# Attention that normalises its outputs instead of its probabilities, and adds its band mask in the scores' own number type, in a two-layer hybrid backbone

## The chip, the core and the metric

The kernel runs on one core of a Trainium2 chip. A core has a matrix engine (PE in the profile, with PEld for its weight loads), a vector engine (DVE), a scalar engine (ACT), a general engine (POOL) and a queue engine for transfers (SP). Each engine works through its own list of instructions in the order in which the program wrote them, and waits for the others by semaphores. The metric is the time of one execution in device microseconds (us); less is better.

## The reference, cut to what matters

The program computes two layers over 256 latent and 256 context tokens with 1024 features. Both mix tokens by attention with 64 features per head: the first layer with 8 query heads (beside a state-space branch, S5), the second with 16 query heads in a band of 128 positions, with a sink logit per head that takes part in the sum of the softmax alone. What the change touches is the softmax with its values:

```
def gqa_scores(q5, k):
    s = jnp.einsum('bqkgd,bskd->bkgqs', q5, k, preferred_element_type=jnp.float32)
    return s * (HEAD_DIM ** -0.5)

def gqa_values(p, v):
    return jnp.einsum('bkgqs,bskd->bqkgd', p.astype(v.dtype), v)

def sink_softmax(s, sink):
    sk = jnp.broadcast_to(sink.astype(jnp.float32)[:, :, None, None], s.shape[:-1] + (1,))
    p = jax.nn.softmax(jnp.concatenate([s, sk], axis=-1), axis=-1)
    return p[..., :-1]
...
    valid = (kpos >= 0) & (kpos < n) & (jnp.abs(kpos - qpos) <= WINDOW)
    ...
        s_loc = jnp.where(mi, gqa_scores(qi, ki), -jnp.inf)
```

## The kernel before, in words

Nearly all large products are done three times, on halves of a split: a number is kept as a rounded high part (type fp32r) and a remainder, and `mm3` (L390) multiplies high by high, high by low and low by high. The program runs feed-forward, mixer, feed-forward for each layer. Weights come by transfers on SP, and ACT and DVE split them (L281, L299) one use ahead. The order on each engine is the order in which the Python code writes instructions; there is no scheduler. Pieces of side work are generators in a list `bg`, and each call of `tick()` writes the next piece of each.

**Attention** (L915) is called twice, with 8 units each. A unit is 128 queries and two neighbouring query heads for each of two key heads; its two key heads are its two subs, so there are 16 subs. A loop of steps handles sub after sub, with stages three steps apart. At step s it writes:
- `scores` of sub s: for two heads a product with the high and one with the low part of the keys (L934, L937), into one of four buffers of the accumulator memory, and in the second layer between them a bf16 product of an identity with a mask of 128 columns (L936); then a maximum on DVE (L938);
- `transposes` of sub s-3 on PE (L985), copied out by ACT (L986);
- `softmax` of sub s: the maximum scaled on DVE (L950), two exponentials on ACT with their sums (L958); then, for sub s-1, the inverse of the sums on DVE (L970) and the scaling of the two probability tiles: in the first layer one on ACT (L973) and one on POOL (L975), in the second one on DVE and one on POOL (both L975);
- `values`, at each odd step from 5 on, of the unit whose two subs are transposed: products of values and probabilities into `po` (L995), whose result DVE copies and splits into high and low part, head by head (L999, L1000);
- `tick()`, which in the first layer brings the S5 branch: products on PE (L1469, L1546), a rotation on POOL (L1497 to L1503), scans and products on DVE (L1514 to L1528), copies on ACT (L1472, L1557).

The context queries of the first layer see 256 keys, all others 512, so that a tile of scores there is 256 columns wide for subs 0 to 7 and 512 for the rest. After the attention comes the output projection (`pwo`).

The mask tiles are made once, early in the program, on POOL (`win_masks`, L821). The second layer's mixer (`mixer_win`, L1758) begins with products for keys and values (`pkv`), while the norm of its input is still being made: ACT, DVE and POOL write the operand tiles `hh` and `hl` feature block by feature block, and POOL raises the mean squares to the power -1/2 (L530), which PE spreads over the partitions (L534).

Of the kernel before, what the change touches and what calls it, by code (L numbers as in the profile page):

```python
# [11 lines left out]
F32 = mybir.dt.float32  # L12
# [24 lines left out]
def hybrid_kernel(ctx: ExitStack, tc: tile.TileContext, x, c, ctx_in, c_ctx, mod_w, mod_b, norm_g, ffn_wg, ffn_wu,  # L37
# [66 lines left out]
    def ps(name, tag="mm", shape=(128, 512)):  # L104
        return psum.tile(list(shape), F32, name=name, tag=tag, bufs={"mm": 4, "tp": 2, "ms": 2}[tag])

    def tt(name, shape, tag=None, bufs=2, dtype=F32):
        return tmp.tile(list(shape), dtype, name=name, tag=tag or name, bufs=bufs)
# [58 lines left out]
    class Operand:  # L167
# [11 lines left out]

        def __getitem__(self, ix):  # L180
            return self.t[ix[2] // 4][ix[:2] + (ix[2] % 4,) + ix[3:]]

    hh, hl = Operand("hh"), Operand("hl")

# [3 lines left out]
    def tokens(t):  # L188

        return t // 2, slice((t % 2) * 128, (t % 2 + 1) * 128)  # L190
# [624 lines left out]
                G.tensor_mul(ropeS[:, z, :, hs], rp[:, :, 32:64], gains[:, l, z, None, ho].to_broadcast([128, 2, 32]))  # L815
            G.tensor_scalar(ropeS[:, z, :, 0:32], ropeS[:, z, :, 0:32], -1.0, None, op0=OP.mult)

    masks = const.tile([128, 3, 128], BF16, name="masks")
    sinkb = const.tile([128, 2, 16], F32, name="sinkb")

    def win_masks():  # L821

        mf = tt("mf", [128, 2, 128], tag="half", bufs=3)
        G.memset(mf, 0.0)
        G.affine_select(mf[:, 0], mf[:, 0], pattern=[[-1, 128]], base=0, channel_multiplier=1,
                        compare_op=OP.is_ge, fill=NEG)
        G.affine_select(mf[:, 1], mf[:, 1], pattern=[[1, 128]], base=0, channel_multiplier=-1,
                        compare_op=OP.is_ge, fill=NEG)
        G.tensor_copy(masks[:, 0:2], mf)
        G.tensor_copy(masks[:, 2], ident)  # L830
        G.tensor_scalar(sinkb[:, 1], sinkb[:, 0], -1.0, None, op0=OP.mult)

    scr = const.tile([128, 1], F32, name="scr")

# [80 lines left out]
    def attention(ap, units, qT, rq, kTh, kTl, v, dst, pt_slots, mask=None, sinkb=None):  # L915


        subs = [(u, kvl) for u in range(len(units)) for kvl in range(2)]
        state = {}
        pt_n = [0]  # L920

        def scores(u, kvl):
            qcol, kvp, hg0, nkb, msk = units[u]
            nk = nkb * 128
            kv = kvp * 2 + kvl
            l = 0 if sinkb is None else 1
            assert ("q", l, (kv * 4 + hg0) // 8 * 8, qcol.start) in ready
            assert all(("k", l, b * 128) in ready for b in range(nkb))
            scs = []
            mx = tt("mx", [128, 8], bufs=3)  # L930
            for i in range(2):
                h = kv * 4 + hg0 + i
                sc = ps("sc")
                T.matmul(sc[:, 0:nk], qT[:, h, qcol], kTh[:, kv, 0:nk], start=True, stop=False)  # L934
                if msk is not None:
                    T.matmul(sc[:, msk[1] * 128:(msk[1] + 1) * 128], mask[:, 2], mask[:, msk[0]], start=False, stop=False)  # L936
                T.matmul(sc[:, 0:nk], qT[:, h, qcol], kTl[:, kv, 0:nk], start=False, stop=True)  # L937
                V.tensor_reduce(mx[:, i:i + 1], sc[:, 0:nk], axis=AX.X, op=OP.max)  # L938
                scs.append(sc)
            state[u, kvl] = [scs, mx, None]  # L940

        def softmax(u, kvl, prev):

            if (u, kvl) in state:
                qcol, kvp, hg0, nkb, msk = units[u]
                nk = nkb * 128
                scs, mx, _ = state[u, kvl]
                hs = slice((kvp * 2 + kvl) * 4 + hg0, (kvp * 2 + kvl) * 4 + hg0 + 2)
                rqu = rq[:, qcol.start // 128]
                V.tensor_mul(mx[:, 2:4], mx[:, 0:2], rqu[:, 1, hs])  # L950
                if sinkb is not None:
                    V.tensor_tensor(mx[:, 2:4], mx[:, 2:4], sinkb[:, 1, hs], op=OP.min)
                    G.tensor_add(mx[:, 4:6], mx[:, 2:4], sinkb[:, 0, hs])
                sm = tt("smx", [128, 8], bufs=3)
                P = []
                for i in range(2):
                    p = xt_("P", [128, 512])
                    S.activation(p[:, 0:nk], scs[i][:, 0:nk], AF.Exp, bias=mx[:, 2 + i:3 + i],  # L958
                                 scale=rqu[:, 0, hs.start + i:hs.start + i + 1],
                                 accum_out=sm[:, i:i + 1])  # L960
                    P.append(p)
                if sinkb is not None:
                    S.activation(sm[:, 2:4], mx[:, 4:6], AF.Exp)
                state[u, kvl] = [P, sm]
            if prev in state:
                P, sm = state[prev]
                nk = units[prev[0]][3] * 128
                if sinkb is not None:
                    V.tensor_add(sm[:, 0:2], sm[:, 0:2], sm[:, 2:4])
                V.reciprocal(sm[:, 4:6], sm[:, 0:2])  # L970
                for i in range(2):
                    if sinkb is None and i == 0:
                        S.activation(P[i][:, 0:nk], P[i][:, 0:nk], AF.Copy, scale=sm[:, 4:5])  # L973
                        continue
                    (G if i else V).tensor_scalar(P[i][:, 0:nk], P[i][:, 0:nk], sm[:, 4 + i:5 + i], None, op0=OP.mult)  # L975

        def transposes(u, kvl):
            P, sm = state[u, kvl]
            nkb = units[u][3]
            pts = pt_slots[pt_n[0] % len(pt_slots)]  # L980
            pt_n[0] += 1
            for i in range(2):
                pt = ps("ppt", "tp")
                for kb in range(nkb):
                    T.transpose(pt[:, kb * 128:(kb + 1) * 128], P[i][:, kb * 128:(kb + 1) * 128], ident)  # L985
                S.copy(pts[:, 0:nkb, i * 128:(i + 1) * 128], pt[:, 0:nkb * 128].rearrange("p (b q) -> p b q", b=nkb))  # L986
            state[u, kvl] = pts

        def values(u):
            qcol, kvp, hg0, nkb, msk = units[u]  # L990
            po = ps("po", "ms")
            for kb in range(nkb):
                for kvl in range(2):
                    kv = kvp * 2 + kvl
                    T.matmul(po[kvl * 64:kvl * 64 + 64, 0:256], v[:, kb, kv * 64:kv * 64 + 64], state[u, kvl][:, kb, :],  # L995
                             start=kb == 0, stop=kb == nkb - 1, tile_position=(0, kvl * 64))
            for i in range(2):
                hi, lo = dst(u, i)
                V.tensor_copy(hi, po[:, i * 128:(i + 1) * 128])  # L999
                V.tensor_sub(lo, po[:, i * 128:(i + 1) * 128], hi.bitcast(F32))  # L1000

        n = len(subs)
        l = 0 if sinkb is None else 1
        TL, dp, sf = TLS[l], DP[l], SF[l]
        for s_ in range(n + TL):
            if s_ < n and sf:
                scores(*subs[s_])
            if s_ >= TL:
                transposes(*subs[s_ - TL])
            if s_ < n and not sf:  # L1010
                scores(*subs[s_])
            c_ = s_ - dp
            if 0 <= c_ <= n:
                softmax(*(subs[c_] if c_ < n else (-1, 0)), subs[c_ - 1] if c_ else None)
            if s_ >= TL + 2 and (s_ - TL) % 2 == 0:
                values(subs[s_ - TL - 2][0])
            tick()
        values(subs[n - 1][0])


# [12 lines left out]
    def s5_prep(pp):  # L1033
# [44 lines left out]
        for _ in range(6):  # L1078
            yield
        rope_tables(0)  # L1080
        win_masks()
        ee = pt_("ee", [128, 1])
        G.memset(ee, math.e)
        dP = pt_("dP", [32, 2])
# [338 lines left out]
    def mixer_ab(nm, ap, nxt):  # L1423
# [220 lines left out]
        for t in range(4):  # L1644
            s_, tl = tokens(t)
            pq = ps("pq")
            for i in range(2):
# [6 lines left out]
                if i:  # L1654
# [3 lines left out]

        units = [(slice(qt * 128, (qt + 1) * 128), 0, hg0, 4 if qt >= 2 else 2, None) for qt in range(4) for hg0 in (0, 2)]
        attention(ap, units, qT, rq, kTh, kTl, v,  # L1660
                  lambda u, i: tuple(z[:, u // 4, 4 + units[u][2] + i, tokens(u // 2)[1]] for z in (hh, hl)),
                  [z[:, s_] for z in (hh.renew(0, F32), hl.renew(0, F32)) for s_ in (CTX, LAT)])
        gc = ap.tile([128, 2, 2, 4, 256], F32R, name="gc", tag="big")

# [93 lines left out]
    def mixer_win(nm, ap, nxt):  # L1758
# [2 lines left out]
        v = ap.tile([128, 4, 256], F32, name="v1")  # L1761
        qT = ap.tile([128, 16, 256], F32R, name="qT1")
        rq = ap.tile([128, 2, 2, 16], F32, name="rq1")
        ckv = [use(("wkv", 0), pre=MW == 0 or WA == 0)]
        pk = [ps("pkv1") for _ in range(4)]
        for s_ in (CTX, LAT):
# [34 lines left out]
                        tick()  # L1801
        if WX:
            warm(AF.Exp)
        units = [(slice(qt * 128, (qt + 1) * 128), kvp, hg0, 4, (0, 3) if qt == 0 else (1, 2))
                 for kvp in range(2) for qt in range(2) for hg0 in (0, 2)]
        attention(ap, units, qT, rq, kTh, kTl, v,
                  lambda u, i: tuple(z[:, LAT, units[u][1] * 4 + units[u][2] + i, units[u][0]] for z in (hh, hl)),
                  [ap.tile([128, 4, 256], F32, name="pts%d" % i) for i in range(4)], mask=masks, sinkb=sinkb)
        fsl = [slice(0, 128), slice(128, 256)]
        for dp in range(4):  # L1810
# [169 lines left out]
```

## Time and profile before

| What | Value |
|---|---|
| time, median of 3 runs | 1765.51 us (1764.81 to 1765.52) |
| the profiled execution's own time | 1764.46 us |
| its span, first to last instruction | 1762.7 us |
| busy: PE, DVE, ACT, POOL | 1710.7, 1081.6, 633.7, 423.6 us |
| mean granted clock of PE | 0.984 of full speed |

A busy PE is not PE at its peak: matmuls overlap, so two starts one behind the other tell what a matmul costs, rather than its duration. The first attention lies at about 518 to 607 us of the span, the second at about 1479 to 1539 us.

### The profile page before, as it was taken

The numbers are of one execution on the slowest core, as the hardware profiler recorded it, in microseconds if no ns is written. First come the engines' busy times: TensorE is split into PE (matmuls) and PEld (weight loads), VectorE is DVE, ScalarE is ACT, GpSimd is POOL, SyncE is SP. The second block draws the span as 40 slices with busy tenths as digits, with TensorE's granted clock in tenths as the row PEclk, the third lists the DMA queues.
The fourth block names the chain that finished last, engine by engine and source line by source line (L and its number), as shares of the span: only waits on it lengthen the run. The fifth ranks groups of instructions, "written<-read, shape, count | busy, mean of one in ns | idle before, by whom it ended". The sixth has DMA issues, their size and how long they took to land.

```text
span 1762.7 us, 25223 instructions
## 1 busy us (share of the span) xinstructions
PE 1710.7 (97%) x9951; PEld 1432.0 (81%) x9951; DVE 1081.6 (61%) x1802; ACT 633.7 (36%) x1210; POOL 423.6 (24%) x565
## 2 busy tenths in 40 slices
PE   6999999999987999999999999999999998999998
PEld 4778888878975689888888898888888886699998
DVE  5565767666578755576556554754546378755455
ACT  3322222223445643222222243222222357754443
POOL 5314779322367303000000022000000046620000
PEclk8999999999998899999999999999999999999999
DMA  8546575596534524464445323554645224045653
GB/s 262 183 139 174 160 210 178 178 295 215 162 114 162 136 77 165 150 203 135 158 137 165 107 94 114 161 180 146 212 149 166 92 96 96 1 144 169 205 176 120
DMA packets 209453, 272.60 MB, mean 155 GB/s; under 512 B 23672, under 2 KB 171384, under 8 KB 208824
## 3 DMA queue, kind: packets, MB, share of 16 engines
q1 hardware_dynamic: 204912, 261.26, 47.0%
q10 hardware_dynamic: 3064, 5.32, 0.8%
q0 software_dynamic: 1360, 4.42, 0.8%
q8 instruction: 78, 1.28, 0.3%
q14 instruction: 39, 0.32, 0.1%
HBM read 255.77 MB, written 15.17 MB: 154 GB/s over the span
## 4 chain that ended last, share of the span: by engine, by line
PE 84%; DVE 7%; ACT 3%; DMA 3%; issue 2%; POOL 1%; SPq 0%; ACTq 0%; POOLq 0%; DVEq 0%
PE pu L391 16%; PE pu L392 15%; PE pu L393 15%; PE pd L391 7%; PE pd L392 6%; PE pd L393 6%; PE pwo L391 1%; PE pwo L393 1%; PE pwo L392 1%; PE pm L452 1%; PE pacc L391 1%; PE pacc L392 1%; PE pacc L393 1%; DVE H L1528 1%; PE po L995 1%
## 5 line engine op out<-in xcount | busy, mean ns | idle before, releaser
L391 PE MATMUL pu<-hh,whi 128*128 128x512 f32 (+1 forms) x1392 | 505.2, 363 | 1.5 <-ACT hh L548 1.1
L392 PE MATMUL pu<-hl,whi 128*128 128x512 f32 (+1 forms) x1392 | 500.7, 360 | 2.6 <-DVE hl L550 2.6
L393 PE MATMUL pu<-hh,wlo 128*128 128x512 f32 (+1 forms) x1392 | 500.2, 359 | 0.0
L299 DVE TENSOR_TENSOR wlo<-raw,whi 128x1024 fp32r<-128x1024 f32 (+2 forms) x314 | 358.2, 1181 | 42.5 <-ACT whi L281 42.1
L281 ACT CAST whi<-raw 128x1024 fp32r<-128x1024 f32 (+1 forms) x310 | 294.0, 998 | 244.4 <-PE pd L392 160.6
L391 PEld LDWEIGHTS pu<-hh,whi 128*128 128x128 f32 x1392 | 263.5, 189 | 49.6 <-issue 5.3
L392 PEld LDWEIGHTS pu<-hl,whi 128*128 128x128 f32 x1392 | 263.6, 189 | 41.2 <-DVE hl L550 3.4
L393 PEld LDWEIGHTS pu<-hh,wlo 128*128 128x128 f32 x1392 | 263.4, 189 | 39.3 <-DVE wlo L299 0.2
L505 POOL TENSOR_TENSOR acc<-acc,sq 128x256 f32<-128x256 f32 x54 | 41.9, 780 | 784.5 <-ACT sq L511 784.1
L391 PE MATMUL pd<-ahi,whi 128*128 128x512 f32 (+1 forms) x624 | 224.8, 360 | 0.0
L597 DVE TENSOR_TENSOR hm<-sg,pu 128x512 f32<-128x512 f32 (+1 forms) x88 | 54.3, 618 | 274.8 <-PE pu L393 274.6
L393 PE MATMUL pd<-ahi,wlo 128*128 128x512 f32 (+1 forms) x624 | 222.6, 357 | 0.0
L392 PE MATMUL pd<-alo,whi 128*128 128x512 f32 (+1 forms) x624 | 222.6, 357 | 0.0
L226 ACT CAST ahi<-hm 128x512 fp32r<-128x512 f32 (+1 forms) x88 | 49.9, 567 | 366.8 <-DVE hm L597 366.8
L484 DVE SCALAR_TENSOR_TENSOR ma<-mraw,silc,ma 128x1024 f32<-128x1024 f32 (+1 forms) x126 | 142.3, 1160 | 5.1 <-DMA mraw<-in_mod_w_dram 4.8
L391 PEld LDWEIGHTS pd<-ahi,whi 128*128 128x128 f32 x624 | 117.9, 189 | 20.8 <-issue 3.3
L588 DVE SCALAR_TENSOR_TENSOR xT<-pd,m,xT 128x256 f32<-128x256 f32 x192 | 84.7, 478 | 77.7 <-PE pd L393 77.4
L393 PEld LDWEIGHTS pd<-ahi,wlo 128*128 128x128 f32 x624 | 117.9, 189 | 17.5 <-DVE wlo L299 0.4
L392 PEld LDWEIGHTS pd<-alo,whi 128*128 128x128 f32 x624 | 118.0, 189 | 16.4
L593 ACT ACTIVATE sg<-pu 128x512 f32<-128x512 f32 (+1 forms) x88 | 47.5, 544 | 229.8 <-PE pu L393 229.3
L227 DVE TENSOR_TENSOR alo<-hm,ahi 128x512 fp32r<-128x512 f32 (+1 forms) x88 | 55.9, 635 | 55.7 <-ACT ahi L226 55.7
L548 ACT ACTIVATE hh<-h,m 128x256 fp32r<-128x256 f32 x88 | 41.5, 502 | 59.6 <-DVE h L541 59.6
(375 smaller groups left out, 2455.9 us busy)
## 6 DMA issues: line engine op xcount, KB each, us to landing
raw<-in_ffn_wg_dram SPq DMA_DIRECT2D x44, 1024.0 KB, 5.4
raw<-in_ffn_wu_dram SPq DMA_DIRECT2D x44, 1024.0 KB, 5.5
mraw<-in_mod_w_dram SPq DMA_DIRECT2D x72, 512.0 KB, 5.3
raw<-in_mod_w_dram SPq DMA_DIRECT2D x32, 1024.0 KB, 5.1
raw<-in_ffn_wd_dram SPq DMA_DIRECT2D x36, 768.0 KB, 4.6
raw<-in_ffn_wd_dram SPq DMA_DIRECT2D x17, 1024.0 KB, 5.0
raw<-me_d SPq DMA_DIRECT2D x8, 768.0 KB, 5.0
raw<-in_win_w_in_dram SPq DMA_DIRECT2D x6, 1024.0 KB, 5.2
```

The costliest lines, as they stand in the source:

```text
L226: (S.copy if eng is None else eng.tensor_copy)(dst_hi, src)
L227: V.tensor_sub(dst_lo, src, dst_hi.bitcast(F32))
L281: S.copy(ph, src)
L299: eng.tensor_sub(pl_, src, ph.bitcast(F32))
L391: T.matmul(o, lhs[0], rhs[0], start=start, stop=False)
L392: T.matmul(o, lhs[0], rhs[1], start=False, stop=False)
L393: T.matmul(o, lhs[1], rhs[0], start=False, stop=stop)
L484: V.scalar_tensor_tensor(ma[c0, s_], raw[i], silc[:, k, s_:s_ + 1], ma[c0, s_], op0=OP.mult, op1=OP.add)
L505: G.tensor_add(acc[s_], acc[s_], sq_late.pop(s_))
L588: V.scalar_tensor_tensor(xT[:, d, sl], psrc, m[:, l, j, d, s_:s_ + 1], xT[:, d, sl], op0=OP.mult, op1=OP.add)
L593: S.activation(sg, pg, AF.Silu)
L597: V.tensor_mul(hm, sg, pu)
```

## The change

Four things change. The probabilities are no longer scaled: `softmax` only keeps the inverse sums, in a tile `inv` for each unit. `values` first spreads them: four products with an identity put the inverse sum of each query into the 64 partitions of its head, beside the place of `po`; they are copied out to `rb` (by ACT in the first layer, by DVE in the second), and when the values' products are done, DVE multiplies both heads' result by it (L1007), the high part is copied from that (ACT in the first layer, DVE in the second, L1010), and POOL makes the low part (L1011). The mask becomes fp32r, 256 columns wide with a block of zeros, and is added by an fp32r product. And the mask tiles are made at the start of the second layer's mixer instead of early in the program.

```diff
-    def win_masks():
-
-        mf = tt("mf", [128, 2, 128], tag="half", bufs=3)
+    def win_masks(ap):
+
+        mf = ap.tile([128, 2, 128], F32, name="mf", tag="pts3")
         G.memset(mf, 0.0)
...
-        G.tensor_copy(masks[:, 0:2], mf)
-        G.tensor_copy(masks[:, 2], ident)
-        G.tensor_scalar(sinkb[:, 1], sinkb[:, 0], -1.0, None, op0=OP.mult)
+        masks = ap.tile([128, 4, 128], F32R, name="masks")
+        for i in range(2):
+            G.tensor_copy(masks[:, 2 - 2 * i], mf[:, i])
+        G.tensor_scalar(masks[:, 1], ident, 0.0, None, op0=OP.mult)
+        G.tensor_copy(masks[:, 3], ident)
+        return masks
...
-                    T.matmul(sc[:, msk[1] * 128:(msk[1] + 1) * 128], mask[:, 2], mask[:, msk[0]], start=False, stop=False)
+                    T.matmul(sc[:, 256:512], mask[:, 3], mask[:, msk:msk + 2], start=False, stop=False)
...
-                V.reciprocal(sm[:, 4:6], sm[:, 0:2])
-                for i in range(2):
-                    if sinkb is None and i == 0:
-                        S.activation(P[i][:, 0:nk], P[i][:, 0:nk], AF.Copy, scale=sm[:, 4:5])
-                        continue
-                    (G if i else V).tensor_scalar(P[i][:, 0:nk], P[i][:, 0:nk], sm[:, 4 + i:5 + i], None, op0=OP.mult)
+                if prev[1] == 0:
+                    inv[prev[0]] = tt("inv", [128, 2, 2], bufs=4)
+                V.reciprocal(inv[prev[0]][:, prev[1]], sm[:, 0:2])
...
+            r = inv.pop(u)
+            for i in range(2):
+                for kvl in range(2):
+                    T.matmul(po[kvl * 64:kvl * 64 + 64, 256 + i * 128:384 + i * 128], r[:, kvl, i:i + 1].to_broadcast([128, 64]),
+                             ident, start=True, stop=True, tile_position=(0, kvl * 64))
+            rb = tt("rb", [128, 256], tag="acc%d" % (u % 2), bufs=1)
+            (S.copy if sinkb is None else V.tensor_copy)(rb, po[:, 256:512])
...
-            for i in range(2):
-                hi, lo = dst(u, i)
-                V.tensor_copy(hi, po[:, i * 128:(i + 1) * 128])
-                V.tensor_sub(lo, po[:, i * 128:(i + 1) * 128], hi.bitcast(F32))
+            o = tt("ao", [128, 256], tag="h", bufs=2)
+            V.tensor_mul(o, po[:, 0:256], rb)
+            o = o.rearrange("p (i q) -> p i q", i=2)
+            hi, lo = dst(u)
+            (S.copy if sinkb is None else V.tensor_copy)(hi, o)
+            G.tensor_sub(lo, o, hi.bitcast(F32))
...
+        masks = win_masks(ap)
```

Three places show what stands where. First DVE in the first attention, at the odd step that ends unit 3 (`mx` is the maximum, `smx` and `inv` the inverse sums, `po` the values' result, `ao` the scaled result, `uu` and `rhoT` belong to the S5 scan). Before:

```order
L938 TENSOR_REDUCE mx<-sc 128x1 [waits PE_49] x2
L950 TENSOR_TENSOR mx<-mx,rq 128x2 [waits DVE_49]
L970 RECIPROCAL smx<-smx 128x2 [waits Activation_49,Pool_49]
L999 CAST hh_105<-po 128x128 [waits PE_49]
L1000 TENSOR_TENSOR hl_107<-po,hh_105 128x128 [waits DVE_49]
L999 CAST hh_105<-po 128x128
L1000 TENSOR_TENSOR hl_107<-po,hh_105 128x128 [waits DVE_49]
L1514 SCALAR_TENSOR_TENSOR uu<-rhoT,uu 128x256 [waits Pool_49]
```

DVE at the same place, after the change:

```order
L944 TENSOR_REDUCE mx<-sc 128x1 [waits PE_49] x2
L956 TENSOR_TENSOR mx<-mx,rq 128x2 [waits DVE_49]
L977 RECIPROCAL inv<-smx 128x2 [waits Activation_49]
L1007 TENSOR_TENSOR ao<-po,rb 128x256 [waits PE_49,Activation_49]
L1525 SCALAR_TENSOR_TENSOR uu<-rhoT,uu 128x256 [waits Pool_49]
```

Four instructions that waited for PE alone have become one that waits for PE and ACT, in front of the same scan. Second, ACT at the same step after the change (`P` are the exponentials, `ppt` transposed probabilities, `hh_105` the high part of the result):

```order
L988 COPY hh_4989<-ppt 128x4x128 [waits PE_49] x2
L964 ACTIVATE P,smx<-sc,mx,rq 128x512 [waits DVE_49]
L964 ACTIVATE P,smx<-sc,mx,rq 128x512
L1000 COPY rb<-po 128x256 [waits PE_49]
L1010 CAST hh_105<-ao 128x2x128 [waits DVE_49]
```

Before, a scaling of a probability tile (L973) stood behind the two exponentials; now the copy of `rb` and the high part stand there. Third, POOL at the start of the second layer's mixer after the change (`rr` is the inverse root of the mean squares, `h` and `hl` the norm's tiles):

```order
L557 TENSOR_TENSOR hl_107<-h,hh_105 128x256 [waits PE_49,Pool_49]
L827 MEMSET mf 128x256 [waits DMAHW4_49,DMAHW3_49,DMAHW5_49,DMAHW2_49,DMAHW6_49,DMAHW1_49,DMAHW7_49,DMAHW0_49,PE_49]
L828 AFFINE_SELECT mf<-mf 128x128 [waits Pool_49]
L830 AFFINE_SELECT mf<-mf 128x128
L834 CAST masks<-mf 128x128 [waits Pool_49] x2
L835 TENSOR_SCALAR masks<-ident 128x128
L836 CAST masks<-ident 128x128
L534 TENSOR_TENSOR rr<-rs,mhalf 128x2 [waits DVE_49]
L556 TENSOR_TENSOR h<-h,m 128x256 [waits Activation_49]
```

The seven instructions of the masks now stand between a norm's low part (L553 before) and the power -1/2 (L530 before), which followed one another.

## Rows read from the trace of the kernel before

**Rows 1.** The page's chain that ended last, shares by engine.
```profile
PE 84%; DVE 7%; ACT 3%; DMA 3%; issue 2%; POOL 1%; SPq 0%; ACTq 0%; POOLq 0%; DVEq 0%
```
**Rows 2.** Stretch of the first attention: busy PE, PEld, DVE, ACT, POOL, clock.
```profile
575.00:590.00 15.00, 14.65 (x110) 11.58 (x112) 14.62 (x37) 9.84 (x22) 10.56 (x10) 0.80 0.36 97
```
**Rows 3.** One unit of the second attention, the same columns.
```profile
1518.40:1524.60 6.20, 6.20 (x46) 4.20 (x45) 5.56 (x18) 5.31 (x16) 3.90 (x5) 1.00 0.00 0
```
**Rows 4.** DVE timeline, first attention: start, us, line, out<-in, [idle before].
```profile
547.93 0.26 DVE L999 CAST hh<-po 128x128 fp32r<-128x128 f32 x1
...
548.96 0.75 DVE L938 TENSOR_REDUCE mx<-sc 128x1 f32<-128x256 f32 x2
...
563.94 0.29 DVE L999 CAST hh<-po 128x128 fp32r<-128x128 f32 x1 [1.85 <-PE po L995]
...
575.12 0.27 DVE L999 CAST hh<-po 128x128 fp32r<-128x128 f32 x1
...
576.15 0.68 DVE L1514 TENSOR_TENSOR_SCAN uu<-rhoT,uu 128x256 f32<-128x256 f32 x1
```
**Rows 5.** ACT timeline, first attention.
```profile
549.14 0.50 ACT L973 ACTIVATE P<-P,smx 128x256 f32<-128x256 f32 x1
...
576.73 0.74 ACT L973 ACTIVATE P<-P,smx 128x512 f32<-128x512 f32 x1
...
600.38 2.00 ACT L281 CAST whi<-raw 128x1024 fp32r<-128x1024 f32 x2
```
**Rows 6.** ACT and DVE timelines, operations like the new ones, elsewhere.
```profile
1439.77 0.37 ACT L1783 COPY v<-pkv 128x256 f32<-128x256 f32 x1 [0.50 <-PE pkv L393]
...
1442.08 0.42 DVE L849 TENSOR_TENSOR hy<-pkv,gains 128x256 f32<-128x256 f32 x1 [0.33 <-ACT hsq L846]
```
**Rows 7.** PE timeline, first attention: the S5 products and the last transposes.
```profile
547.57 0.61 PE L1546 MATMUL py<-raw,H 128*64 128x128 f32 x8
548.01 0.39 PE L1546 MATMUL py<-raw,U 128*64 128x128 f32 x4
...
601.52 0.39 PE L1546 MATMUL py<-raw,U 128*64 128x128 f32 x4
...
602.94 1.09 PE L985 MATMUL ppt<-ident,P 128*128 128x128 f32 x8
```
**Rows 8.** POOL timeline, start of the second layer's mixer.
```profile
1433.83 0.84 POOL L553 TENSOR_TENSOR hl<-h,hh 128x256 fp32r<-128x256 f32 x1
1435.10 0.71 POOL L530 TENSOR_TENSOR rr<-rs,mhalf 128x2 f32<-128x2 f32 x1 [0.43 <-DVE rs L528]
```
**Rows 9.** PE timeline at that place.
```profile
1435.86 0.43 PE L534 MATMUL pn<-ident,rr 128*128 128x128 f32 x2
```
**Rows 10.** Stretch of the mask tiles before the change (columns as in rows 2).
```profile
32.26:33.85 1.59, 1.31 (x13) 0.75 (x15) 0.17 (x1) 0.00 (x0) 1.45 (x6) 1.00 0.58 138
```
**Rows 11.** PE timeline, scores of the second attention.
```profile
1508.76 0.40 PE L934 MATMUL sc<-kTh,qT 128*128 128x512 f32 x1
1509.00 0.23 PE L936 MATMUL sc<-masks 128*128 128x128 bf16 x1
1509.04 0.48 PE L937 MATMUL sc<-kTl,qT 128*128 128x512 f32 x1
1509.36 1.04 PE L985 MATMUL ppt<-ident,P 128*128 128x128 f32 x8
```
**Rows 12.** PE timeline, scores of 256 columns in the first attention.
```profile
533.28 0.28 PE L934 MATMUL sc<-kTh,qT 128*128 128x256 f32 x1
533.40 0.28 PE L937 MATMUL sc<-kTl,qT 128*128 128x256 f32 x1
```
**Rows 13.** One DVE line of the S5 scan: minimum, median, maximum in ns.
```profile
L1524 DVE TENSOR_TENSOR t<-uu,tbl x16: 411/419/956, 507.7 to 591.5; 128x256 f32<-128x256 f32 x16
```
**Rows 14.** POOL and DVE timelines, a scaling and what ran beside it.
```profile
571.78 1.83 POOL L975 TENSOR_SCALAR P<-P,smx 128x512 f32<-128x512 f32 x1 [2.29 <-DVE smx L970]
...
571.85 0.42 DVE L1524 TENSOR_TENSOR t<-uu,tbl 128x256 f32<-128x256 f32 x1
```

More of the change, by code (lines that the diff above doesn't have):

```diff
@@ L181, in __getitem__, with pair @@
             return self.t[ix[2] // 4][ix[:2] + (ix[2] % 4,) + ix[3:]]
+        def pair(self, s_, k, tok):
+            return self.t[k // 4][:, s_, k % 4:k % 4 + 2, tok]
     hh, hl = Operand("hh"), Operand("hl")
@@ L816, in rope_tables @@
             G.tensor_scalar(ropeS[:, z, :, 0:32], ropeS[:, z, :, 0:32], -1.0, None, op0=OP.mult)
-    masks = const.tile([128, 3, 128], BF16, name="masks")
     sinkb = const.tile([128, 2, 16], F32, name="sinkb")
-    def win_masks():
-        mf = tt("mf", [128, 2, 128], tag="half", bufs=3)
+    def win_masks(ap):
+        mf = ap.tile([128, 2, 128], F32, name="mf", tag="pts3")
         G.memset(mf, 0.0)
@@ L918, in attention @@
         subs = [(u, kvl) for u in range(len(units)) for kvl in range(2)]
-        state = {}
+        state, inv = {}, {}
         pt_n = [0]
@@ L966, in softmax @@
                 P, sm = state[prev]
-                nk = units[prev[0]][3] * 128
                 if sinkb is not None:
                     V.tensor_add(sm[:, 0:2], sm[:, 0:2], sm[:, 2:4])
-                V.reciprocal(sm[:, 4:6], sm[:, 0:2])
-                for i in range(2):
-                    if sinkb is None and i == 0:
-                        S.activation(P[i][:, 0:nk], P[i][:, 0:nk], AF.Copy, scale=sm[:, 4:5])
-                        continue
-                    (G if i else V).tensor_scalar(P[i][:, 0:nk], P[i][:, 0:nk], sm[:, 4 + i:5 + i], None, op0=OP.mult)
+                if prev[1] == 0:
+                    inv[prev[0]] = tt("inv", [128, 2, 2], bufs=4)
+                V.reciprocal(inv[prev[0]][:, prev[1]], sm[:, 0:2])
         def transposes(u, kvl):
@@ L1080, in s5_prep @@
         rope_tables(0)
-        win_masks()
+        G.tensor_scalar(sinkb[:, 1], sinkb[:, 0], -1.0, None, op0=OP.mult)
         ee = pt_("ee", [128, 1])
@@ L1660, in mixer_ab @@
         attention(ap, units, qT, rq, kTh, kTl, v,
-                  lambda u, i: tuple(z[:, u // 4, 4 + units[u][2] + i, tokens(u // 2)[1]] for z in (hh, hl)),
+                  lambda u: tuple(z.pair(u // 4, 4 + units[u][2], tokens(u // 2)[1]) for z in (hh, hl)),
                   [z[:, s_] for z in (hh.renew(0, F32), hl.renew(0, F32)) for s_ in (CTX, LAT)])
@@ L1803, in mixer_win @@
             warm(AF.Exp)
-        units = [(slice(qt * 128, (qt + 1) * 128), kvp, hg0, 4, (0, 3) if qt == 0 else (1, 2))
+        units = [(slice(qt * 128, (qt + 1) * 128), kvp, hg0, 4, 1 - qt)
                  for kvp in range(2) for qt in range(2) for hg0 in (0, 2)]
         attention(ap, units, qT, rq, kTh, kTl, v,
-                  lambda u, i: tuple(z[:, LAT, units[u][1] * 4 + units[u][2] + i, units[u][0]] for z in (hh, hl)),
+                  lambda u: tuple(z.pair(LAT, units[u][1] * 4 + units[u][2], units[u][0]) for z in (hh, hl)),
                   [ap.tile([128, 4, 256], F32, name="pts%d" % i) for i in range(4)], mask=masks, sinkb=sinkb)
```

## The prediction

> **What bounds the kernel now.** I began with the chain of work that ended last: PE holds 84% of it and DVE 7% [rows 1]. So an operation costs time where PE is the one waited for, or where the chain leaves PE. I then read the two attentions in stretches, since the change lies there. In the first attention DVE is the full engine: 14.62 of 15 us from 575 to 590 us, while POOL and ACT have a third of it free [rows 2]. PE looks full too, but its clock is at 0.80 there and it waits several times for ACT, which waits for DVE. The reader is to see that from about 530 to 595 us DVE's queue sets the pace, and that only the last two units, when DVE has run dry, are paced by PE. In the second attention it is the reverse: a unit takes 6.20 us and PE is busy for 6.20, DVE for 5.56, ACT for 5.31 and POOL for 3.90 [rows 3]. Freed time on DVE and POOL there buys nothing; added time on PE is paid in full. The third place is the start of the second layer's mixer: POOL finishes a low part at 1433.83 + 0.84 = 1434.67 us, raises the norm's power from 1435.10 to 1435.81 [rows 8], and PE spreads it at 1435.86 [rows 9], which is the moment it is ready. PE is therefore already waiting for POOL at this spot.
>
> **First attention: a wait on DVE.** Before, the four copies of a result stood on DVE right behind the inverse and waited for nothing but PE. For unit 0 they began at 547.93 and the next maximum at 548.96, so they took 1.03 us; for unit 3 they ran from 575.12 to 576.15, again 1.03 us, with no idle time in front [rows 4]. Now one multiplication stands there and needs `rb`. `rb` is copied by ACT behind the two exponentials of the same step, and these need the maximum that DVE has only just made. So DVE must stand still while ACT does two exponentials and the copy. ACT was through with the exponentials when its scaling began: 549.14 and 576.73 us [rows 5]. The copy of 128x256 out of the accumulator memory I price at 0.37, and the multiplication of such a tile with one from SBUF at 0.42, after operations of the same form [rows 6]; the hand-over is 0.05 by my reading. Unit 0: 549.14 + 0.37 + 0.05 + 0.42 = 549.98 against 548.96, so 1.0 us later. Unit 3: 576.73 + 0.84 = 577.57 against 576.15, so 1.4 us later. Behind the multiplication are queued the scans of S5 and the next maximum, for which ACT and then PE wait, so on a full DVE this is passed on. Units 0 and 1 have exponentials of 256 columns (1.0 each), units 3 and 4 of 512 (1.4 each). For unit 2 DVE already waited 1.85 us for PE [rows 4], so I take 0.5, between nothing and 1.4. Together 2.0 + 0.5 + 2.8 = 5.3 us.
>
> The last two units are paced by PE. The spreading is four products of 128 columns into 64 partitions. S5's products have this very form: eight instructions, which are four products of full-precision numbers, from 547.57 to 548.01, so 0.44 us [rows 7]. Two units add 0.9; for the earlier ones DVE is the cover. ACT loses a scaling of 0.74 before the copies that PE then waits for, which I count as 0.6 back, since neighbours on ACT overlap a little. But ACT's weight casts, 2.00 us from 600.38 [rows 5], were out of the way 0.56 us before PE's last transposes at 602.94 [rows 7]. Now they stand behind the high part of unit 6, about 0.9 us after its products (multiplication, copy, hand-overs), and end 2.9 after them, while PE needs ACT's copy of its last transposes some 1.9 us after them (1.4 of S5 products, 602.94 - 601.52 [rows 7], and half the transposes) and has the spreading of 0.44 in between: about 0.7 of wait, an estimate from these rows. Sum of the end: 0.9 - 0.6 + 0.7 = 1.0. First attention: **+6.3 us**.
>
> What POOL gains and gives I count as nothing, between -2 and +2: its scalings (1.83 us for 512 columns [rows 14]) go, and low parts (0.84 [rows 8]) come, which stand in front of its S5 rotations. A DVE line of S5 takes 0.42 us mostly and up to 0.96 [rows 13], so a POOL neighbour can cost DVE about 0.54 per operation; but the one started 0.07 us after POOL's scaling took 0.42 [rows 14], so the scalings that go were not the dear neighbour. The Trainium skill's page "SBUF — State Buffer" says in its section "SBUF: two separate sides" that a GpSimd operation that reads SBUF and a VectorE operation with two SBUF inputs lock each other out for a whole instruction. By this rule the scalings' removal would give DVE much back and the sum would come out near the second rival below; this row does not agree with it for the scaling.
>
> **Second layer's start: POOL in PE's way.** The mask tiles are made between the low part and the power. Before, five operations took the 1.59 us of their stretch [rows 10], some 0.3 each; now there are seven (one wide copy became two narrow ones, a zero block and a scaling came), so about 2.2 us as an estimate. POOL is free at 1434.67, the power then starts at 1436.87 and not at 1435.10: +1.8 us [rows 8]. PE's spreading stands in order, and the products behind it wait with it [rows 9]. Nothing hides this: **+1.8 us**, from 1.3 (operations as short as before) to 2.5. Taking the masks out of the early program, where PE has feed-forward work, I count at nothing; POOL's early work is done long before its use.
>
> **Second attention: PE.** Each of 8 units gets the spreading of 0.44 us: **+3.5 us**. Lower bound this, upper bound the duration of 0.61 [rows 7]: 4.9. The mask: before, the bf16 product took 0.04 (1509.00 to 1509.04), but the product behind it took 0.32 (to 1509.36), against 0.24 for the one before (1508.76 to 1509.00) [rows 11]: a change of number type cost 0.08, together 0.12. Now an fp32r product of 256 columns takes 0.12 [rows 12] and the one behind it should take 0.24: no change. The upper end is a product as dear as one of 512 columns, 0.24, so 32 x 0.12 = 3.8 more; no row suggests less than 0.12. DVE and POOL lose their scalings, and nothing is won by it, since PE has no gap [rows 3]. `rb` is on DVE here and is copied while PE does the products. At the end the low part now comes from POOL, but the output projection has 18 products of 0.12 (2.2 us) on other features first, which covers the multiplication, a copy and the low part, 0.42 + 0.37 + 0.84; uncovered it would cost 0.8.
>
> **Sum.** 6.3 + 1.8 + 3.5 = +11.6 us. The profiled execution took 1764.46 us, so 1776.1; it lies 1.05 us below the median of the three runs, which the range covers. A measurement of this kernel can tell about 0.2% (3.5 us) from no change.
>
> **Rivals.**
> - *DVE's wait is hidden* (chance 0.2). The S5 work and ACT's freed scalings let the maximum and exponentials run ahead, so that the 5.3 us vanish. For it: the 1.85 us that DVE waited at unit 2. Against: a queue in order cannot pass the multiplication. 1764.5 + 1.0 + 1.8 + 3.5 = 1771.
> - *Faster, by DVE's relief* (chance 0.1). If POOL's scalings did hold DVE, the 12 of them in the stretch that DVE paces would each give back one or two times 0.54 us, 6.5 to 13; then with the waits of 5.3 gone as above, the sum is 6.3 (end, masks, second attention) less that: 1764 to 1758, and I name 1758, where each scaling covers two operations. It decides from 0.8 us of relief for each scaling. Against it stands the row of 0.42 beside a scaling.
> - *Dearer on PE* (chance 0.1). Mask and spreading at their upper ends: 11.6 + 3.8 + 1.4, so 1781.
>
> **How the numbers follow.** My forecast has 0.6. It and the two rivals above 1770 end slower; of the first rival and of the forecast's lower end I give 0.06 to within 0.2%, and the faster rival splits into 0.08 faster and 0.02 the same. So 0.08 faster, 0.08 same, 0.84 slower. The forecast's own range runs from the lower bounds (POOL's relief -2, waits of unit 2 none, masks -0.5) at 1773 to the upper at 1781. The range that should hold 8 in 10 leaves out the faster rival and a tenth at the ends: 1767 to 1782.
>
> **What would show it.** In the first attention the multiplication on DVE should show idle time of 1.5 to 2 us in front of it, ended by ACT's `rb`, and DVE less than 14.6 of 15 us busy. At the mixer's start PE's spreading of the norm should show about 2 us of idle time ended by POOL. In the second attention a unit should take 6.64 us with PE full, and the mask's product and the one behind it 0.12 and 0.24. I am wrong if DVE's multiplication starts right behind the inverse, if S5's DVE lines fall to 0.42 throughout, or if PE does not wait for the power.

## The result and the profile after

The changed kernel takes 1810.55 us (median of 4 runs, 1810.35 to 1811.58) against 1765.16 for before (4 runs, 1764.49 to 1765.52). The ratio is 1.0257, with a 95% interval of 1.0245 to 1.0269: slower by 45 us, where 11 were forecast. The direction was right and the size wrong by a factor of four.

First the page of the changed kernel: span, busy time of the engines, and the chain that ended last, which answers to [rows 1].

```profile
span 1808.6 us, 25353 instructions
...
PE 1729.8 (96%) x10079; PEld 1444.3 (80%) x10079; DVE 1074.0 (59%) x1754; ACT 631.7 (35%) x1210; POOL 388.1 (21%) x551
...
PE 83%; DVE 8%; ACT 3%; DMA 3%; issue 2%; POOL 1%; SPq 0%; DVEq 0%; POOLq 0%; ACTq 0%
```

DVE, ACT and POOL have less to do than before, and the span is 45.9 us longer all the same. So the reader looks for waits, PE's first. Two views of who PE waited for: the first attention (515 to 640 us), then 1400 to 1600 us, each with us in total, times and the longest.

```profile
PE po L1004 <- ACT rb L1000: 29.1, 8, 6.7
PE py L1557 <- DVE H L1539: 6.4, 1, 6.4
```
```profile
PE po L1004 <- DVE rb L1000: 4.8, 8, 1.1
PE pqt L887 <- ACT qT L889: 3.0, 1, 3.0
PE pn L538 <- POOL rr L534: 1.7, 1, 1.7
```

The wait for `H` (6.4) and that for `qT` (3.0) are there before too. New are the 34 us in which the values' products wait for `rb`, once in each of 16 units, and the 1.7 us for POOL's power. PE's timeline shows the shape of the first: start, duration, line, operands, and in brackets the idle time with what ended it.

```profile
545.77 1.12 PE L997 MATMUL po<-ident,inv 128*64 128x128 f32 x8
553.57 1.98 PE L1004 MATMUL po<-hh,v 128*64 128x256 f32 x8 [6.68 <-ACT rb L1000]
...
563.90 1.08 PE L1004 MATMUL po<-hl,v 128*64 128x256 f32 x8 [1.33 <-ACT rb L1000]
...
589.28 1.97 PE L1004 MATMUL po<-hl,v 128*64 128x256 f32 x8 [5.95 <-ACT rb L1000]
```

ACT's and DVE's timelines say why `rb` was so late: it stands behind the exponentials, and these behind DVE's queue.

```profile
552.06 0.56 ACT L964 ACTIVATE P<-sc,mx,rq 128x256 f32<-128x256 f32 x1 [1.22 <-DVE inv L977]
...
552.61 0.56 ACT L964 ACTIVATE P<-sc,mx,rq 128x256 f32<-128x256 f32 x1
...
553.15 0.37 ACT L1000 COPY rb<-po 128x256 f32<-128x256 f32 x1
```
```profile
551.88 0.16 DVE L977 RECIPROCAL inv<-smx 128x2 f32<-128x2 f32 x1
555.67 0.42 DVE L1007 TENSOR_TENSOR ao<-po,rb 128x256 f32<-128x256 f32 x1 [3.63 <-PE po L1004]
```

PE spread the sums by about 547 us and then stood until 553.57. The products do not use `rb`, but they write columns 0 to 255 of the tile `po`, and ACT reads columns 256 to 511 of the same tile. The program holds PE until that read is done. The Trainium skill gives a reason for such a wait on the page "PSUM — Partial Sum Buffer", in the section "PSUM bank collisions raise a hardware error": a write by TensorE and a read by ScalarE or VectorE may not meet in one bank and quadrant, disjoint columns included, so they are to be kept apart by bank and quadrant and not by address. The trace agrees with that order in all 16 units; no run here lets the two meet. The order of instructions had shown it too, in PE's list (before, then after; the first values' products of the first attention):

```
L995 MATMUL po<-hh_5000,v 64x256 x4
...
L1004 MATMUL po<-hh_4989,v 64x256 [waits Activation_49]
```

The second attention, a unit from one start of the products to the next (columns as in [rows 3]), and the power at the start of the second layer's mixer, on POOL and on PE:

```profile
1542.12:1549.45 7.33, 6.80 (x52) 5.17 (x53) 4.87 (x15) 5.28 (x16) 1.12 (x3) 1.00 0.00 0
```
```profile
1468.15 0.83 POOL L557 TENSOR_TENSOR hl<-h,hh 128x256 fp32r<-128x256 f32 x1
1468.93 0.31 POOL L827 MEMSET mf<- 128x256 f32 x1
...
1471.05 0.72 POOL L534 TENSOR_TENSOR rr<-rs,mhalf 128x2 f32<-128x2 f32 x1
```
```profile
1471.83 0.43 PE L538 MATMUL pn<-ident,rr 128*128 128x128 f32 x2 [1.71 <-POOL rr L534]
```

A unit is 1.13 us longer than the 6.20 of [rows 3], and PE is idle for 0.53 of it. The seven mask instructions take 2.12 us (1471.05 - 1468.93), and PE waits 1.71, near the 1.8 that was priced.

One more loss lies where the change has no instruction: in the feed-forward. This view keeps shapes apart: line, operands, count, then busy us and mean ns of one. The products of the down projection with 512 columns, after the change:

```profile
L395 PE MATMUL pd<-ahi,whi 128*128 128x512 f32 x432 | 172.0, 398 | 0.0
L397 PE MATMUL pd<-ahi,wlo 128*128 128x512 f32 x432 | 170.7, 395 | 0.0
L396 PE MATMUL pd<-alo,whi 128*128 128x512 f32 x432 | 170.6, 395 | 0.5 <-DVE alo L231 0.5
```

And before:

```profile
L391 PE MATMUL pd<-ahi,whi 128*128 128x512 f32 x432 | 169.8, 393 | 0.0
L393 PE MATMUL pd<-ahi,wlo 128*128 128x512 f32 x432 | 168.3, 390 | 0.0
L392 PE MATMUL pd<-alo,whi 128*128 128x512 f32 x432 | 168.3, 390 | 0.0
```

That is 5 ns each, 1296 times, 6.5 us. The 264 like products of the last feed-forward (`pacc`) are 4 to 6 ns longer as well, 1.2 us.

### The profile page after: what moved, and what is told of

Its sections match the earlier page's. It is cut to its first block, busy times and chain, and to the rows that moved or that the text cites. A ratio compares the mean times of both kernels' runs of the same rounds, so it can differ in the third digit from the quotient of the medians.

```text
span 1808.6 us, 25353 instructions
## 1 busy us (share of the span) xinstructions
PE 1729.8 (96%) x10079; PEld 1444.3 (80%) x10079; DVE 1074.0 (59%) x1754; ACT 631.7 (35%) x1210; POOL 388.1 (21%) x551
## 4 chain that ended last, share of the span: by engine, by line
PE 83%; DVE 8%; ACT 3%; DMA 3%; issue 2%; POOL 1%; SPq 0%; DVEq 0%; POOLq 0%; ACTq 0%
PE pu L395 15%; PE pu L396 15%; PE pu L397 15%; PE pd L395 7%; PE pd L397 6%; PE pd L396 6%; PE po L1004 2%; DVE mx L944 2%; PE pwo L396 1%; PE pwo L395 1%; PE pwo L397 1%; PE pm L456 1%; PE pacc L397 1%; PE pacc L396 1%; PE pacc L395 1%
```

## The experiments

Seventeen kernels ran. Each difference is taken against runs of before on the same chip (medians 1764.9 to 1766.2).

**1. The order inside `values`.** Only the order is turned: the products first, then the spreading with the copy.

```diff
             po = ps("po", "ms")
-            r = inv.pop(u)
...
-            (S.copy if sinkb is None else V.tensor_copy)(rb, po[:, 256:512])
             for kb in range(nkb):
...
+            r = inv.pop(u)
...
+            (S.copy if sinkb is None else V.tensor_copy)(rb, po[:, 256:512])
```

> Against the changed kernel, only the order inside values is turned: first the products of values and probabilities, then the spreading and the copy to rb. Theory (the products stand behind the copy rb, since both use one tile of the accumulator memory, and rb stands behind two exponentials on ACT): PE's idle time ended by rb goes, 20 us come back in the first attention (26.3 lost there now, 6.3 by the sum on record) and 8 x 0.53 in the second, 1810.5 - 24 = 1786. Rival (the wait is passed on: DVE's multiplication, then the next maxima and exponentials come just as late): less than 10 us come back in the first attention, 1796 or more.

Measured 1787.75, ratio 1.0132 (1.0115 to 1.0149): 22.8 us come back, as the theory had it. No product waits for `rb` any more, and now the wait appears that the prediction had priced, 1.5 to 2.0 us in five of the eight units of the first attention and 2.5 to 5.2 in the other three. DVE's timeline, two of the five:

```profile
552.90 0.42 DVE L1007 TENSOR_TENSOR ao<-po,rb 128x256 f32<-128x256 f32 x1 [1.52 <-ACT rb L1005]
...
582.97 0.42 DVE L1007 TENSOR_TENSOR ao<-po,rb 128x256 f32<-128x256 f32 x1 [1.89 <-ACT rb L1005]
```

**2. The two parts of the change, and the place of the tiles.** The masks alone, the normalisation alone, and the changed kernel with 768 bytes of constants put back.

```diff
+    pad = const.tile([128, 3, 128], BF16, name="pad")
+    V.memset(pad, 0.0)
     sinkb = const.tile([128, 2, 16], F32, name="sinkb")
```

> The kernel before with the new masks alone (fp32r product of 256 columns, tiles made at the start of the second layer's mixer). Theory: +1.7 for the power that POOL raises later, 32 products at -0.02 each, -0.6, and if the wider spacing of the feed-forward products (7.4 us over the program) comes from tiles that lie at other addresses since the masks left the constants, +7.4: 1773.7. Rival (that spacing belongs to the other part of the change or to the run): 1766.3.

> The changed kernel with the masks of before (bf16, made early among the constants): the normalisation behind the values' products alone. Theory: first attention +26.3, second +9.0, feed-forward as before since the constants are as before: 1765.2 + 35.3 = 1800.5. Rival (the feed-forward's wider spacing belongs to this part): 1808.

> The changed kernel with an unused constant tile of 768 bytes per partition in the place that the masks left, so that the later tiles lie where they lay before. Theory (addresses set the spacing of the feed-forward products): 7.4 us back, 1803. Rival (no effect of addresses): 1810.5, with products of the feed-forward as far apart as in the changed kernel.

Masks alone: 1768.49, ratio 1.0019 (1.0009 to 1.0028), 2.2 us above the rival's number, with the feed-forward as before; the theory that the constants' room sets its spacing fell. Normalisation alone: 1809.1 (1.0253), the rival's number. Pad: 1811.95 (1.0272), no effect, and the down products are at 398 ns still. So nearly everything, the feed-forward's loss too, belongs to the normalisation. That part brings one new tile, `inv`, into the pool of temporary tiles, behind which the pool of `ahi` and `alo` is laid out. This was tried next.

**3. Addresses by themselves.** Before, with an unused tile of 64, 128 or 256 bytes in that pool; and "products first" with `inv` four times as wide.

```diff
         state = {}
+        pad = tt("pad", [128, 16], bufs=1)
+        V.memset(pad, 0.0)
```
```diff
-                    inv[prev[0]] = tt("inv", [128, 2, 2], bufs=4)
+                    inv[prev[0]] = tt("inv", [128, 2, 8], bufs=4)
```

> The kernel before with nothing but an unused tile of 64 bytes per partition in the pool of temporary tiles (and two short writes to it), as large as the new tile inv. Theory (the feed-forward's down products are further apart because their operand tiles, in a pool behind that one, lie 64 bytes further on): pd products at 0.233 us instead of 0.227, as in the changed kernel, and about 9 us more: 1774. Rival (addresses do nothing, the spacing comes with the changed instructions): 1765 and 0.227.

> The order products first, spreading behind, and inv made four times as wide, so that its four buffers take 256 bytes and not 64. Theory of addresses: pd products back at 0.227 us, 1787.75 - 9 = 1778.5, which is the sum on record (+11.6) but for 2 us. Rival: 1787.8 and 0.233.

> The kernel before with an unused tile of 128 bytes per partition in the pool of temporary tiles. Where 64 bytes gave pd products at 0.229 us and +3.5 us, the four buffers of inv may have taken 128. Theory of addresses: 0.233 us and +7.5, 1772.5, as between products first with inv narrow and wide. Rival (it grows no further or falls back): 1765 to 1769.

> The same with 256 bytes. Theory of addresses (only what is left of a multiple of 256 counts, as the wide inv showed): pd products at 0.227 us and the time of before, 1765.2. Rival (any shift of the later tiles costs): 1769 or more.

The ratios: 64 bytes 1.0021 (1.0012 to 1.0030), 128 bytes 1.0049 (1.0034 to 1.0065), 256 bytes 1.0001 (0.9992 to 1.0010). With `inv` wide the changed order falls from 1787.75 to 1780.28, ratio 1.0084 (1.0071 to 1.0097). The down products of before plus 64, of before plus 128, and of products first with `inv` wide:

```profile
L391 PE MATMUL pd<-ahi,whi 128*128 128x512 f32 x432 | 170.9, 396 | 0.0
L393 PE MATMUL pd<-ahi,wlo 128*128 128x512 f32 x432 | 169.7, 393 | 0.0
L392 PE MATMUL pd<-alo,whi 128*128 128x512 f32 x432 | 168.4, 390 | 0.0
```
```profile
L391 PE MATMUL pd<-ahi,whi 128*128 128x512 f32 x432 | 172.0, 398 | 0.0
L393 PE MATMUL pd<-ahi,wlo 128*128 128x512 f32 x432 | 170.7, 395 | 0.0
L392 PE MATMUL pd<-alo,whi 128*128 128x512 f32 x432 | 170.5, 395 | 0.0
```
```profile
L395 PE MATMUL pd<-ahi,whi 128*128 128x512 f32 x432 | 169.8, 393 | 0.0
L397 PE MATMUL pd<-ahi,wlo 128*128 128x512 f32 x432 | 168.3, 390 | 0.0
L396 PE MATMUL pd<-alo,whi 128*128 128x512 f32 x432 | 168.3, 390 | 0.0
```

A kernel whose only new work is two short writes loses 8.7 us (0.0049 of 1765.4) by 128 bytes of room and nothing by 256. That addresses set the spacing is shown. That 64 bytes cost as much as the change was wrong: they slow the products of `ahi` by 3 ns and leave those of `alo`. The changed kernel's rows are those of 128 bytes; the built program bears this out: it lays the four buffers of `inv`, 16 bytes each, 32 bytes apart, so that they take 128 in all. The 768 bytes of experiment 2 are three times 256, which fits their having no effect.

**4. `rb` earlier, and in a tile of its own.** The spreading and the copy at the start of the step (7); in the first attention alone, `inv` wide (8); the spreading in its own tile at the old place (9); own tile, start of the step, high part on DVE, first attention alone (10).

```diff
+            if s_ >= TL + 2 and (s_ - TL) % 2 == 0:
+                spread(subs[s_ - TL - 2][0])
             if s_ < n and sf:
                 scores(*subs[s_])
```
```diff
+            pr = ps("pr", "ms")
...
-            (S.copy if sinkb is None else V.tensor_copy)(rb, po[:, 256:512])
+            (S.copy if sinkb is None else V.tensor_copy)(rb, pr[:, 0:256])
```

> The changed kernel, its order spreading, rb, products kept, but spreading and rb written at the start of the step, ahead of its scores, transposes and softmax; the products stay where they were. Theory (what was late was rb behind two exponentials on ACT, and behind two maxima on DVE in the second attention): neither PE nor the multiplication waits for rb any more; first attention +1 against before, second +2.8, the down products still at 0.233: 1783. Rival (what holds PE is the shared tile as such): PE still waits for rb, 1800 or more.

> The normalisation behind the values in the first attention alone, with spreading and rb at the start of the step and inv of 256 bytes; second attention and masks as before. Theory: five units paced by DVE each save 0.6 us there (four copies of 1.03 become a multiplication of 0.42), 3.0; PE pays 0.44 for each of the last two units and ACT's casts at the end stand behind the high part, +1.6; 1764.9 - 1.4 = 1763.5. Rival (the freed time on DVE is not passed on): +1.6, 1766.5.

> The changed kernel, its order kept, but the spreading writes a tile of its own, from the same two buffers as po. Theory (what binds PE to ACT is that rb is read from the tile that the products write): the products start right behind the spreading, as with the products put first: 1787, between 1784 and 1792, the multiplication on DVE waiting for rb 1.5 to 2 us as there. Rival (the two buffers, shared with the S5 branch, now make PE wait instead): 1795 or more.

> First attention alone, second attention and masks as before, inv of 256 bytes; the spreading in a tile of its own and, with rb, at the start of the step, and the high part on DVE. Theory (both waits for rb gone, DVE 0.3 us less per unit, PE 0.44 more for each of the last two): within 0.2% of before, 1765. Rival (the third tile in the two buffers binds PE to ACT's late copies): 1770 or more.

Measured 1788.66 (1.0134), 1775.85 (1.0059), 1792.16 (1.0152), 1775.92 (1.0053). Earlier helps, and less than expected: in run 7 PE still waits for `rb` 14.3 us in five units of the first attention, since ACT is then still at the exponentials of the step before. An own tile is one more user of the two buffers that `po` shares with S5: in run 9 PE still waits 8.0 us for `rb` at its values' products, of 29.1 in the changed kernel, and 5.4 for S5's `Ssb`. PE's waits in run 10, 515 to 622 us:

```profile
PE sc L938 <- ACT P L962: 5.8, 2, 3.0
PE po L1015 <- ACT Ssb L1503: 5.2, 1, 5.2
PE pr L1003 <- ACT yt L1588: 4.2, 1, 4.2
PE po L1015 <- ACT yt L1588: 2.8, 2, 2.0
PE po L1015 <- ACT rb L1006: 1.8, 1, 1.8
```

The wait for `rb` is nearly gone and PE waits for S5's copies instead (`Ssb`, `yt`; before, 3.9 for `yt` and none for `Ssb`). Run 10 came out as its rival said, and 9 lies on the border of its theory. Run 8 missed both its theory (1763.5) and its rival (1766.5) by over 9 us: PE waits for `rb` there as in run 7, 15.0 us in five units, which neither had counted.

**5. Who copies `rb` and the high part.** From products first with `inv` wide, in the first attention: `rb` on DVE (13), the high part on DVE (14), both (15), both in the first attention alone (16), and `rb` on DVE there alone (17).

```diff
-            (S.copy if sinkb is None else V.tensor_copy)(rb, po[:, 256:512])
+            V.tensor_copy(rb, po[:, 256:512])
...
-            (S.copy if sinkb is None else V.tensor_copy)(hi, o)
+            V.tensor_copy(hi, o)
```

> Products first and inv wide, and rb copied by DVE in the first attention too (a copy of 0.42 behind the spreading). Theory (of the 9.7 us that the first attention still loses, 5.4 up to its last scores are DVE's waits for ACT's rb): these waits go, five copies of 0.42 come, 1780.3 - 3.3 = 1777. Rival (that loss is PE's spreading, or DVE now waits for PE as long): 1780 to 1782.

> Products first and inv wide, and the high part made by DVE in the first attention too. Theory (behind its last scores the first attention loses 4.7 us, since ACT's weight casts now stand behind the high part): about 3 of them come back, and the high part adds 0.3 on DVE to each of five units, 1780.3 - 3 + 1.5 = 1778.8. Rival (the casts are not what PE waits for): 1781.8.

> Both: rb and the high part on DVE in the first attention, products first, inv wide. By the sum of the two theories 1780.3 - 3.3 - 1.5 = 1775.5; by the two rivals 1782 or more.

> The same in the first attention alone, second attention and masks as before. Theory: the 4.8 of the second attention and the 1.7 of the power go, 1775.5 - 6.5 = 1769. Rival (with ACT and POOL freed and no wait for ACT the first attention gains on before): within 0.2% of before or below, 1765.

> Products first, rb on DVE, the high part on ACT, inv wide, all in the first attention alone; second attention and masks as before. Theory (in the run with rb on DVE everywhere the first attention lost 2.7 us, all of it behind its last scores; the second attention and the power lost the rest): 1765.5 + 2.7 = 1768. Rival (the freed scalings of ACT and POOL show once the second attention is out of the way): 1765 or less.

Measured 1772.25 (1.0033, 1.0022 to 1.0044), 1783.04 (1.0095), 1777.12 (1.0061), 1770.93 (1.0027) and 1768.02 (1.0013, 1.0004 to 1.0022). `rb` on DVE gives 8 us, more than twice the 3.3 expected. DVE's timeline in run 13, where the copy, the multiplication and the next scan follow without idle time:

```profile
574.88 0.16 DVE L977 RECIPROCAL inv<-smx 128x2 f32<-128x2 f32 x1
574.95 0.40 DVE L1005 COPY rb<-po 128x256 f32<-128x256 f32 x1
575.39 0.43 DVE L1007 TENSOR_TENSOR ao<-po,rb 128x256 f32<-128x256 f32 x1
575.73 1.26 DVE L1525 TENSOR_TENSOR_SCAN uu<-rhoT,uu 128x256 f32<-128x256 f32 x2
```

The high part on DVE makes it slower, by 2.8 and 4.9 us: the theory of the weight casts fell, its rival holds. Runs 15 and 16 ended 1.6 and 1.9 us above the sums of their theories, and 17 at the number of its theory. No version beats the kernel before; the best, 17, is 0.13% behind.

## Why the prediction was wrong, step by step

How late PE is against before at five places of the profiled executions, in us (first attention begins: its first scores; ends: the first product behind its output projection; second attention begins: its keys' first transposes; ends: the first product of the output projection behind it):

| Kernel | first begins | first ends | second begins | second ends | span |
|---|---|---|---|---|---|
| changed | +2.2 | +28.5 | +35.9 | +43.7 | +45.9 |
| products first | +2.8 | +11.5 | +19.0 | +21.9 | +23.0 |
| products first, `inv` wide | +0.8 | +10.5 | +12.4 | +16.0 | +16.5 |
| and `rb` on DVE | -0.3 | +2.4 | +2.7 | +6.3 | +6.6 |

**The step that failed** is the one that let the values' products run beside the copy: "`rb` is on DVE here and is copied while PE does the products", and the like assumption in the first attention, where only DVE's multiplication was made to wait. The products are queued behind the reader of their own tile. In the first attention this costs 17.6 us (28.5 - 2.2 against 11.5 - 2.8): PE, which was ahead of DVE, is bound to ACT's last copy in the step, ACT to DVE's maximum, and DVE again to PE's next scores. A second order view of the same change, PE's, would have shown it; the views that the prediction used were those of DVE, ACT and POOL.

**The first attention's own sum (+6.3)** holds, up to the last scores, for the kernel that it had in mind. With the products first DVE's multiplication waits 1.5 to 2.0 us for `rb`, as "what would show it" said, in five units of eight, and the first attention loses 8.7 (9.7 with `inv` wide). Of the 9.7, 5.4 lie before its last scores, where the sum had 5.3; with `rb` on DVE they are gone. One unit was misjudged on the way: at unit 2 DVE waits 3.7 us where it had waited 1.85, so 1.3 us are lost with the shorter work counted, and not 0.5. Behind the last scores 4.3 us are lost where 1.0 was priced; this term was mis-sized. With `rb` on DVE 2.7 remain there. Of these, two spreadings of 0.44 are the priced part, and where the rest comes from stays open, since moving the high part off ACT did not bring it back.

**The power (+1.8)** came at 1.7. **The mask's product** costs nothing: it starts at 1537.60, the product behind it at 1537.71 and the next scores at 1537.94, so 0.11 and 0.23 where 0.12 and 0.24 were forecast.

**The second attention (+3.5)** lost 7.8. With the products first (and `inv` wide) its unit is the forecast one, 6.60 us with PE full (forecast 6.64):

```profile
1530.72:1537.32 6.60, 6.60 (x54) 5.26 (x53) 4.73 (x16) 5.38 (x15) 1.12 (x3) 1.00 0.00 0
```

From its beginning to its end it then loses 3.0 to 3.6, so this term held for the order that it had in mind. Of the 1.13 that the changed kernel adds to a unit, 0.53 is the wait for `rb` and 0.60 the spreading, which costs 0.40 where the next products follow it at once.

**Not in the sum at all** was the place of tiles: about 7.5 us (1787.75 - 1780.28), by the rows 6.5 + 1.2 = 7.7. No row of before could have shown it, as no instruction there changes.

**The rivals.** DVE's wait was not hidden, and the scalings that left POOL gave DVE no relief: the S5 line of [rows 13] takes 411, 419 and 951 ns (minimum, median, maximum) after the change. So the rule of the Trainium skill's page "SBUF — State Buffer", section "SBUF: two separate sides", does not show here for the scalings, as the row before had it. Over the first attention of before, the S5 products L1523 and L1524 take 0.88 to 0.96 us where they start beside one of POOL's rotations (L1497 to L1499), which the change leaves in, and 0.41 to 0.61 where they start beside a scaling. The dearest case, 1781, was meant for another reason, PE's own price; the range to 1782 was missed by 28.6 us mainly by what was left out of the list: the wait, 22.8 us by turning the order, and the place of tiles, 7.5. The kernel without these two takes 1780.28, within the range and above the forecast, by the term that was mis-sized above all.

## What to carry to other kernels

When a result gets a second use of its accumulator tile, read the waits of every later writer of that tile as carefully as those of the reader: an engine that was free to run ahead can be bound by it to the last engine in the step. Write first what waits for least; here turning two groups of lines was worth half the loss. And when a change brings even a small new tile, compare the same unchanged instructions in both traces by form, since a few ns on a thousand products add up: here to 7.5 us, more than any one term of the forecast.

## What the runs showed of the hardware

How fast the same products follow one another depends on where their operands lie. With the pool of `ahi` and `alo` shifted by 0, 64, 128 and 256 bytes per partition, the 1296 down products took 393/390/390, 396/390/393, 398/395/395 and 393/390/390 ns on the mean (`ahi` with `whi`, `alo`, `ahi` with `wlo`), all at a granted clock of 1.00 in the feed-forward. Their starts lie 227 ns apart without a shift and 233 with 128 bytes. There the shifted tile is the operand of 512 columns that streams through PE. In the last feed-forward's products (`pacc`) it is the one that is loaded as weights, and they grow as well. The other operand, the split matrix `whi` or `wlo`, keeps its place in both. Before, then before plus 64:

```profile
L391 PE MATMUL pacc<-whi,ahi 128*128 128x512 f32 x88 | 34.4, 390 | 0.0
```
```profile
L391 PE MATMUL pacc<-whi,ahi 128*128 128x512 f32 x88 | 34.9, 396 | 0.0
```

Whether each address counts by itself, or the one against the other, stays open.

A wait on PE can cost more than its length. In the first attention the granted clock was 0.86 before (515 to 612 us) and 0.81 after (515 to 640). In the changed kernel's fourth unit the spreading still ran at 1.00 (582.67 to 583.30 us). Then PE stood for 5.95 us, and the eight instructions of products behind the wait ran at the lower of the two levels (1.2 GHz), 0.50, and took 1.97 us. The same eight before, with no wait in front of them, ran at 1.00 and took 1.08. Before, then a stretch after the change (columns as in [rows 2]):

```profile
570.01 1.08 PE L995 MATMUL po<-hl,v 128*64 128x256 f32 x8
```
```profile
589.28:591.20 1.92, 1.92 (x9) 0.78 (x9) 0.00 (x0) 0.00 (x0) 0.00 (x0) 0.50 0.00 0
```

Not every slow product stands for this: the products of the first unit took 1.98 us behind the wait of 6.68, but they took 1.98 before as well, and the clock was at 0.50 ahead of that wait already, when the spreading took 1.12.
